# One layer's dense expert stage: every second V block in plain float32 instead of every sixth

## The chip, the cores and the metric

The kernel runs on one core of one Trainium2 chip. The metric is the device time of one execution in microseconds; the median of three runs of the kernel before is 4275.73 (4273.55 to 4280.51).

## What is computed

Two layers of a backbone over 512 latent tokens and 256 context tokens with 1024 features. Each layer has a token mixer and then PEER, a retrieval of small experts; the change touches PEER of the first layer alone. There each token gets, for each of 8 heads, the 16 best of 128 x 128 experts. Their rows of one table give activations, and the activations, weighted by a softmax gate, combine the rows of a second table:

```python
gate = jax.nn.softmax(top_s, axis=-1).astype(xb.dtype)
act = jax.nn.gelu(jnp.einsum('td,thkd->thk', xb, u_tab[eid]))
return jnp.einsum('thk,thkd->td', gate * act, v_tab[eid])
```

Each table has 16384 rows of 1024 floats, 64 MB a layer.

## The kernel before, in words

Tokens of a layer go one of two ways. The **dense** way (`peer_x`, line 1158) takes the first 384 of the 512 latent tokens of layer 0 against all 16384 experts, in 128 blocks of 128 experts. `ublock` (line 1200) loads a block of the transposed first table, multiplies it with the tokens and leaves GELU activations in one of 64 slots (32 in the tile `PA`, 32 in `PB`). `weights` (line 1211) builds one-hot matrices on VectorE and ScalarE, multiplies them on TensorE (tile `pwt`, line 1239), and so multiplies the slots by each token's gate; it is called 144 times in the layer, in three groups of 48. `vblock` (line 1245) loads a block of the second table and adds slot x block to the accumulators `dacc` (three of 128 tokens by 1024). U blocks run 64 ahead of V blocks, so in the stage looked at here one U block follows each of the first 64 V blocks, and the last 64 V blocks stand alone.

The **gather** way (`gtile_u`, line 1101, and `gtile_v`, line 1112) takes the other 128 latent tokens and the 256 context tokens. For each of 128 chosen experts a token, GpSimd issues an indirect load of 128 table rows (512 KB, tile `grow`, five buffers, line 1097); VectorE then multiplies and sums it (line 1108) or adds it to an accumulator (line 1121). One such load with its VectorE step is called a gather here. There are 768 in layer 0, of which 338 lie ahead of V block 0 in VectorE's order.

A float32 product is done in one of two ways. `block` (line 1192) loads 512 KB into `uv` (two buffers) and calls `split` (line 111): ScalarE writes a rounded part `uvh`, VectorE the remainder `uvl` (two buffers each). For a V block `split` is called a second time, for the slot's 384 columns (`wh`, `wl`). `mm` (line 116) then makes three passes of rounded float32 instead of one exact product: 18 matmuls for a V block. This is called a split block here. In a **plain** block (lines 1247 to 1250) nothing is split; `uv` and the slot go to TensorE as they are, with 6 float32 matmuls. A split block gives its `uv` buffer back when VectorE has written `uvl`, a plain block when TensorE has run its matmuls.

The order of the work on each engine is fixed when the kernel is built: a scheduler walks through all instructions by the levels that `prio` gives (line 81: 3 for the dense stage of layer 0, 6 for the gathers), and places them as its own estimates of durations have them come free. Each engine then executes its list in order, and waits where a semaphore is not there yet. Loads of `uv` are issued from SyncE. When the last V block is done, `L1304` and `L1146` write the layer's output for the 384 tokens, and layer 1 begins with a normalization, transposes and the input projection `pwin`.

Of the kernel before, what the change touches and what calls it, by code (L numbers as in the profile page):

```python
# [71 lines left out]
class Kern:  # L72
# [100 lines left out]
    def schedule(self):  # L173
        a = self.a
        with ExitStack() as er:
            ec = ExitStack()
            self.context(ec, 0)
            with self.banks("ctx0", "right", w=2, S=1) as ps, ExitStack() as e0:
                md = e0.enter_context(self.pool("mod", side="right"))
                pm = e0.enter_context(self.banks("mod", "right", w=1))  # L180
                fl = e0.enter_context(self.pool("flt"))
                pf = e0.enter_context(self.banks("flt", "left", w=2, S=1))
                with self.prio(1), ExitStack() as e:
                    self.filters(fl, pf, 0, LC)
                    self.modulation(md, pm, 0, 0, 2)
                    st = self.front(e, ps, ps, 0, 1, 1, side="right")
                    self.filters(fl, pf, 0, LX)
                    self.modulation(md, pm, 0, 2, 6)
                    self.back(ps, ps, 0, 1, st, None)
                    self.filters(fl, pf, 1, LX)  # L190
                    self.modulation(md, pm, 1, 0, 2)
            self.gp = er.enter_context(self.pool("gath", side="right"))
            with self.prio(1), self.banks("rc", "right", w=2) as ps:
                gc = self.route(ps, 0, 1, "GG", side="right")
            with self.banks("x0", "left", w=2, S=2) as ps:
                with ExitStack() as e:
                    with self.prio(3):
                        pr = e.enter_context(self.banks("x0b", "right", w=2))
                        st = self.front(e, ps, pr, 0, 0, 3, split=False)
                        ex = ExitStack()  # L200
                        self.back(ps, pr, 0, 0, st, ex)
                ec.close()
            with self.prio(6):
                self.gtile_u(0, gc[0])
                self.gtile_v(0, 1, 0, gc[0])
                self.gtile_u(0, gc[1])
            with self.prio(3):
                gx, ex = self.peer_x(0, 384, 6, 32, 32, (36, 46, 46), ex)
            with self.prio(6):
                self.gtile_u(0, gx[3])  # L210
                self.gtile_v(0, 0, 3, gx[3])
                self.gtile_v(0, 1, 1, gc[1])
            with ExitStack() as ec, ExitStack() as e:
                self.context(ec, 1)
                ps = e.enter_context(self.banks("x1", "left", w=2, S=2))
                pr = e.enter_context(self.banks("x1b", "right", w=2))
                with self.prio(3):
                    st = self.front(e, ps, pr, 1, 0, 4, ctx=True)
                with self.prio(4):
                    self.back(ps, pr, 1, 0, st, None, (2, 6))  # L220
            with self.prio(5):
                gx, _ = self.peer_x(1, 320, 0, 32, 46, (44, 42, 42), ex)
            with self.prio(6):
                for i in sorted(gx, reverse=True):
                    self.gtile_u(1, gx[i])
                    self.gtile_v(1, 0, i, gx[i])
# [1211 lines left out]
```

## Time and profile before

| | us |
|---|---|
| median of three runs (lowest, highest) | 4275.73 (4273.55, 4280.51) |
| the profiled execution | 4275.16 |
| its span, first to last instruction | 4273.3 |
| TensorE busy | 3707.9 (87%) |
| VectorE busy | 3510.8 (82%) |
| ScalarE busy | 1904.1 (45%) |
| GpSimd busy | 1532.1 (36%) |

The profile tells, for the whole span or for a stretch, how long each engine was busy, which TensorE clock was granted (1.00 is full speed), and the share of time in which the 16 DMA engines moved data. A list in order of time gives start and duration of single instructions, and in brackets how long the engine had been idle and what ended it. Matmuls overlap, so the price of one is the distance between starts.

### The profile page before, as it was taken

How to read it: one execution, taken by the hardware profiler on the slowest of the kernel's cores; microseconds unless marked ns; L12 is line 12 of the kernel's file. 1: busy time of each engine (PE TensorE's matmuls, PEld its weight loads, DVE VectorE, ACT ScalarE, POOL GpSimd, SP SyncE). 2: the span in 40 equal slices, each digit the busy share in tenths (PEclk: the TensorE clock that was granted, in tenths of full speed). 3: DMA queues.
4: the chain of work that ended last, by engine and by line, in shares of the span. 5: the costliest groups of instructions: out<-in, count | busy, mean ns of one | idle time of the engine just before them, and what ended most of it. 6: DMA issues, size and time to landing. Idle time of an engine off the chain costs nothing.

```text
span 4273.3 us, 63792 instructions
## 1 busy us (share of the span) xinstructions
PE 3707.9 (87%) x22514; PEld 2805.8 (66%) x22514; DVE 3510.8 (82%) x7449; ACT 1904.1 (45%) x3719; POOL 1532.1 (36%) x1225
## 2 busy tenths in 40 slices
PE   6887987968978989999969978888888999999997
PEld 3545544558878877877646656447878877776654
DVE  5746988889889889988898875755898998898988
ACT  5544243433257426622552244533334655555632
POOL 0000245642344563366436620000126345553243
PEclk7998998988999999999989989898999999999998
DMA  6654587885767897799879952242459788887697
GB/s 208 211 192 157 202 304 252 286 299 187 257 224 258 311 348 254 249 359 352 286 233 346 342 190 82 92 134 100 136 180 352 265 300 299 287 302 277 226 349 269
DMA packets 305635, 1063.74 MB, mean 249 GB/s; under 512 B 35757, under 2 KB 42625, under 8 KB 305315
## 3 DMA queue, kind: packets, MB, share of 16 engines
q0 software_dynamic: 165888, 604.05, 40.6%
q1 hardware_dynamic: 139426, 455.61, 30.6%
q8 instruction: 177, 2.90, 0.3%
q14 instruction: 144, 1.17, 0.1%
HBM read 1042.69 MB, written 16.84 MB: 248 GB/s over the span
## 4 chain that ended last, share of the span: by engine, by line
PE 32%; DMA 22%; DVE 17%; issue 16%; POOL 7%; ACT 5%; SPq 0%; POOLq 0%; DVEq 0%; ACTq 0%
PE pst L121 7%; POOL grow L1097 7%; DMA grow<-in_peer_v_dram,eid 6%; PE dacc L121 6%; DMA grow<-in_peer_u_dram,eid 6%; DMA uv<-in_peer_ut_dram 4%; PE pwin L121 4%; PE ppq L121 3%; DMA uv<-in_peer_v_dram 3%; DVE uvl L114 3%; DVE acc L1108 2%; DVE acc L1121 2%; PE pwo L121 2%; DMA wmod<-in_w_mod_dram 1%; ACT uvh L113 1%
## 5 line engine op out<-in xcount | busy, mean ns | idle before, releaser
L1097 POOL DMA_INDIRECT grow<-in_peer_u_dram,eid x576 | 747.8, 1298 | 1157.3 <-DVE acc L1108 566.4
L1097 POOL DMA_INDIRECT grow<-in_peer_v_dram,eid x576 | 776.6, 1348 | 746.4 <-DVE acc L1121 601.0
L121 PE MATMUL pst<-dhT,uvh 128*128 128x384 f32 (+1 forms) x4096 | 1001.6, 329 | 0.0
L113 ACT CAST uvh<-uv 128x1024 fp32r<-128x1024 f32 x491 | 513.0, 1045 | 680.5 <-DMA uv<-in_peer_v_dram 411.3
L121 PE MATMUL pst<-dhT,uvl 128*128 128x384 f32 (+1 forms) x2048 | 696.8, 340 | 112.3 <-DVE uvl L114 77.2
L1121 DVE SCALAR_TENSOR_TENSOR acc<-grow,gate,acc 128x1024 f32<-128x1024 f32 x571 | 732.2, 1282 | 53.8 <-DMA grow<-in_peer_v_dram,eid 46.0
L1108 DVE SCALAR_TENSOR_TENSOR acc<-grow,ghx 128x1024 f32<-128x1024 f32 x576 | 704.1, 1222 | 75.3 <-DMA grow<-in_peer_u_dram,eid 68.1
L121 PEld LDWEIGHTS pst<-dhT,uvh 128*128 128x128 f32 x4096 | 733.0, 193 | 4.1 <-issue 1.9
L114 DVE TENSOR_TENSOR uvl<-uv,uvh 128x1024 fp32r<-128x1024 f32 x491 | 599.1, 1222 | 159.5 <-ACT uvh L113 152.9
L121 PEld LDWEIGHTS pst<-dhT,uvl 128*128 128x128 f32 x2048 | 395.8, 193 | 212.3 <-DVE uvl L114 155.5
L121 PE MATMUL dacc<-uvh,wl 128*128 128x512 f32 x1154 | 481.2, 417 | 38.4 <-DVE wl L114 19.1
L121 PE MATMUL dacc<-uvl,wh 128*128 128x512 f32 x1154 | 467.3, 405 | 25.2 <-DVE uvl L114 25.1
L121 PE MATMUL dacc<-uvh,wh 128*128 128x512 f32 x1154 | 462.8, 401 | 0.0
L1235 ACT ACTIVATE o<-iota,di2n 128x128 f16<-128x128 f32 x1056 | 325.6, 390 | 28.8 <-PE pwt L1239 28.5
L121 PEld LDWEIGHTS dacc<-uvh,wl 128*128 128x128 f32 x1154 | 220.3, 191 | 128.4 <-ACT uvh L113 30.6
L121 PEld LDWEIGHTS dacc<-uvl,wh 128*128 128x128 f32 x1154 | 220.6, 191 | 82.7 <-DVE uvl L114 38.3
L121 PEld LDWEIGHTS dacc<-uvh,wh 128*128 128x128 f32 x1154 | 220.8, 191 | 48.3
L1239 PEld LDWEIGHTS <-o 128*128 128x128 f16 x4224 | 126.1, 97 | 110.7 <-issue 32.7
L1239 PE MATMUL pwt<-og,o 128*128 128x46 f16 (+3 forms) x4224 | 152.0, 182 | 43.3 <-DVE og L1225 35.5
L1205 ACT ACTIVATE PA<-pst 128x384 f32<-128x384 f32 (+1 forms) x128 | 59.5, 464 | 281.0 <-PE pst L121 280.9
L1205 ACT ACTIVATE PB<-pst 128x384 f32<-128x384 f32 (+1 forms) x128 | 59.2, 462 | 232.4 <-PE pst L121 231.8
L254 POOL MEMSET rmod<- 128x512 f32 (+1 forms) x8 | 3.3, 417 | 420.3 <-PE lpg L722 99.7
(399 smaller groups left out, 6092.6 us busy)
## 6 DMA issues: line engine op xcount, KB each, us to landing
uv<-in_peer_ut_dram SPq DMA_DIRECT2D x256, 512.0 KB
uv<-in_peer_v_dram SPq DMA_DIRECT2D x256, 512.0 KB
wmod<-in_w_mod_dram SPq DMA_DIRECT2D x96, 512.0 KB
wpq<-in_peer_wq_dram SPq DMA_DIRECT2D x48, 512.0 KB
w_in<-in_w_in_dram SPq DMA_DIRECT2D x72, 256.0 KB
w_in<-in_w_in_dram SPq DMA_DIRECT2D x18, 512.0 KB
grow<-in_peer_u_dram,eid POOLq DMA_INDIRECT x576
grow<-in_peer_v_dram,eid POOLq DMA_INDIRECT x576
```

The costliest lines, as they stand in the source:

```text
L113: self.nc.scalar.copy(hi, src)
L114: self.nc.vector.tensor_tensor(lo, src, hi.bitcast(F32), op=ALU.subtract)
L121: self.nc.tensor.matmul(p, w[i], x[j], start=start and n == 0, stop=stop and n == len(passes) - 1)
L254: nc.gpsimd.memset(r, 0.0)
L1097: self.nc.gpsimd.indirect_dma_start(out=r, out_offset=None, in_=self.a[table], in_offset=bass.IndirectOffsetOnAxis(ap=eid[:, j:j + 1], axi ...
L1108: nc.vector.scalar_tensor_tensor(junk, r, 1.0, hx, op0=ALU.mult, op1=ALU.mult, accum_out=dot[:, j:j + 1])
L1121: nc.vector.scalar_tensor_tensor(acc, r, w[:, j:j + 1], acc, op0=ALU.mult, op1=ALU.add)
L1205: nc.scalar.activation(slot(i), p, AF.Gelu_apprx_tanh)
L1235: nc.scalar.activation(o2[:, q], self.iota, AF.Abs, bias=i2n[:, t, k * NC + q:k * NC + q + 1])
L1239: nc.tensor.matmul(p[:, q, :], o2[:, q, :], og[:, g, q, :], start=(g == 0), stop=(g == 1))
```

## The change

The third argument of `peer_x`, `vn`, goes from 6 to 2 in layer 0. In `vblock` the plain way is taken if `i % vn == vn - 1`: 64 of the 128 V blocks in place of 21. Nothing else is edited.

```diff
             with self.prio(3):
-                gx, ex = self.peer_x(0, 384, 6, 32, 32, (36, 46, 46), ex)
+                gx, ex = self.peer_x(0, 384, 2, 32, 32, (36, 46, 46), ex)
```

The branch that takes the argument is not edited:

```python
if vn and i % vn == vn - 1:
    raw = dn.tile([128, D], F32, name="uv", bufs=2 + l)
    nc.sync.dma_start(raw, a["peer_v"][r0:r0 + 128, :])
    v, w = [raw], [slot(i)]
else:
    raw, v = block("v", a["peer_v"][r0:r0 + 128, :])
    w = [sp.tile([128, nd * 128], F32R, name=n, bufs=2) for n in ("wh", "wl")]
    self.split(*w, slot(i)[:, :nd * 128])
```

The scheduler places other instructions too. On VectorE, around V block 26, where `weights` (L1220, L1231, L1225, L1242) and gathers (L1108) are mixed with the splits (L114), before, from the `wl` of block 26 on:

```order
L114 TENSOR_TENSOR wl<-PA,wh 128x384
L1108 SCALAR_TENSOR_TENSOR acc,dot<-grow,ghx 128x1024
L1242 SCALAR_TENSOR_TENSOR PB<-pwt,PB 128x28x8
L1242 SCALAR_TENSOR_TENSOR PA<-pwt,PA 128x18x8
L1242 SCALAR_TENSOR_TENSOR PB<-pwt,PB 128x28x8
L1242 SCALAR_TENSOR_TENSOR PA<-pwt,PA 128x18x8
L1225 TENSOR_TENSOR og<-o_15149,diT 128x736
L114 TENSOR_TENSOR uvl<-uv,uvh 128x1024
```

and, in the change, a piece of the same place:

```order
L1108 SCALAR_TENSOR_TENSOR acc,dot<-grow,ghx 128x1024
L1225 TENSOR_TENSOR og<-o_14813,diT 128x736
L1108 SCALAR_TENSOR_TENSOR acc,dot<-grow,ghx 128x1024
L1220 TENSOR_TENSOR o_14846<-iotah,diT 128x368
L114 TENSOR_TENSOR uvl<-uv,uvh 128x1024
L1108 SCALAR_TENSOR_TENSOR acc,dot<-grow,ghx 128x1024 x3
L1242 SCALAR_TENSOR_TENSOR PB<-pwt,PB 128x28x8
```

In the change more gathers stand between the same `weights` steps: from V block 26 to V block 28 there were 3 gathers before, and there are 8 now.

On VectorE, at the end of the stage, the last gathers (L1121), splits (L114) and the first steps of the output (L1304, L1146, and L105 of layer 1's normalization), before:

```order
L1121 SCALAR_TENSOR_TENSOR acc<-grow,gate,acc 128x1024 x4
L114 TENSOR_TENSOR uvl<-uv,uvh 128x1024
L1121 SCALAR_TENSOR_TENSOR acc<-grow,gate,acc 128x1024 x3
L1304 TENSOR_TENSOR PA<-dacc_10704,PA 128x1024
L1304 TENSOR_TENSOR PA<-dacc_10705,PA 128x1024
L1146 TENSOR_TENSOR xs<-PA 128x1024 x2
L1304 TENSOR_TENSOR PA<-dacc_10706,PA 128x1024
L1121 SCALAR_TENSOR_TENSOR acc<-grow,gate,acc 128x1024
L1146 TENSOR_TENSOR xs<-PA 128x1024
```

and in the change, from V block 106 to V block 112 (the rows after these, up to `L1304`, are `wl` and `uvl` alone):

```order
L1121 SCALAR_TENSOR_TENSOR acc<-grow,gate,acc 128x1024 x6
L114 TENSOR_TENSOR uvl<-uv,uvh 128x1024
L114 TENSOR_TENSOR wl<-PB,wh 128x384
L1121 SCALAR_TENSOR_TENSOR acc<-grow,gate,acc 128x1024 x5
L1130 TENSOR_TENSOR acc<-acc,grow 128x1024
L114 TENSOR_TENSOR wl<-PB,wh 128x384
L114 TENSOR_TENSOR uvl<-uv,uvh 128x1024
L1146 TENSOR_TENSOR grow<-grow,acc 128x1024
```

The 768th gather of the layer stands ahead of V block 108's `wl` in the change; before, 749 stood ahead of `L1304`, and 19 followed it among the first steps of layer 1.

On SyncE, the loads of `uv` near the end of the stage and what each waits for (L1196 is a split block, L1249 a plain one; DVE is VectorE's `uvl`, PE the last matmul of a plain block), before:

```order
L1249 DMA uv<-in_peer_v_dram 128x1024 [waits DMAHW5_49,DVE_49]
L1196 DMA uv<-in_peer_v_dram 128x1024 [waits DMAHW6_49,DVE_49]
L1196 DMA uv<-in_peer_v_dram 128x1024 [waits DMAHW0_49,DVE_49]
L1196 DMA uv<-in_peer_v_dram 128x1024 [waits DMAHW7_49,PE_49]
L1196 DMA uv<-in_peer_v_dram 128x1024 [waits DMAHW1_49,DVE_49]
```

and in the change:

```order
L1249 DMA uv<-in_peer_v_dram 128x1024 [waits DMAHW3_49,DVE_49]
L1196 DMA uv<-in_peer_v_dram 128x1024 [waits DMAHW2_49,PE_49]
L1249 DMA uv<-in_peer_v_dram 128x1024 [waits DMAHW5_49,DVE_49]
L1196 DMA uv<-in_peer_v_dram 128x1024 [waits DMAHW4_49,PE_49]
L1249 DMA uv<-in_peer_v_dram 128x1024 [waits DMAHW7_49,DVE_49]
```

Every load of a split block now waits for TensorE; before, one in six did.

## Rows read from the trace of the kernel before

**Rows 1.** The page's first line, and busy time by stretch, stretches A to G.

```profile
span 4273.3 us, 63792 instructions
...
core 0: us, PE busy (x) PEld busy (x) DVE busy (x) ACT busy (x) POOL busy (x), PEclk, DMA share, GB/s
1432.60:1629.70 197.10, 173.62 (x831) 143.64 (x831) 163.96 (x250) 59.18 (x90) 123.82 (x92) 0.97 0.95 344
1629.70:1794.70 165.00, 162.89 (x1395) 137.29 (x1394) 156.07 (x324) 116.82 (x257) 53.06 (x41) 1.00 0.70 235
1794.70:2080.90 286.20, 260.15 (x1180) 217.54 (x1179) 243.22 (x262) 80.41 (x109) 188.14 (x135) 0.96 0.95 350
2080.90:2228.40 147.50, 109.71 (x1080) 78.62 (x1078) 141.13 (x278) 101.67 (x239) 32.75 (x34) 0.87 0.69 222
2228.40:2352.20 123.80, 113.00 (x413) 79.77 (x414) 104.46 (x99) 28.59 (x39) 81.10 (x59) 0.96 0.95 344
2352.20:2461.00 108.80, 98.95 (x369) 68.37 (x367) 92.25 (x87) 24.73 (x33) 67.11 (x51) 1.00 0.93 338
2461.00:2510.70 49.70, 19.02 (x69) 14.34 (x68) 48.25 (x75) 24.36 (x54) 19.27 (x20) 0.62 0.77 266
```

**Rows 2.** Stretches A, B, D and G, instructions on gathers alone (tile grow).

```profile
core 0: us, DVE busy (x) ACT busy (x) POOL busy (x), PEclk, DMA share, GB/s
1432.60:1629.70 197.10, 112.07 (x182) 0.00 (x0) 123.82 (x92) 0.97 0.95 344
1629.70:1794.70 165.00, 49.12 (x80) 0.00 (x0) 53.06 (x41) 1.00 0.70 235
...
2080.90:2228.40 147.50, 47.13 (x37) 0.00 (x0) 32.75 (x34) 0.87 0.69 222
...
2461.00:2510.70 49.70, 26.69 (x21) 0.00 (x0) 19.07 (x16) 0.62 0.77 266
```

**Rows 3.** VectorE in order of time, splits and a gather, from 2438.99.

```profile
start us, us, engine line op out<-in xcount [idle before <-releaser]
2438.99 1.22 DVE L114 TENSOR_TENSOR uvl<-uv,uvh 128x1024 fp32r<-128x1024 f32 x1
2440.13 0.55 DVE L114 TENSOR_TENSOR wl<-PB,wh 128x384 fp32r<-128x384 f32 x1
2440.60 1.28 DVE L1121 SCALAR_TENSOR_TENSOR acc<-grow,gate,acc 128x1024 f32<-128x1024 f32 x1
2441.79 0.55 DVE L114 TENSOR_TENSOR wl<-PB,wh 128x384 fp32r<-128x384 f32 x1
```

**Rows 4.** TensorE in order of time: a plain block and what follows; a split block likewise.

```profile
1479.01 5.31 PE L121 MATMUL dacc<-uv,PA 128*128 128x512 f32 x12
...
1484.69 0.33 PE L121 MATMUL pst<-dhT,uvl 128*128 128x384 f32 x1
...
1901.60 0.39 PE L121 MATMUL dacc<-uvh,wl 128*128 128x512 f32 x1
...
1905.81 0.33 PE L121 MATMUL pst<-dhT,uvl 128*128 128x384 f32 x1
...
1906.34 0.35 PE L121 MATMUL pst<-dhT,uvl 128*128 128x384 f32 x1
...
1910.00 5.31 PE L121 MATMUL dacc<-uv,PB 128*128 128x512 f32 x12
```

**Rows 5.** One load of uv, issued on SyncE and met by ScalarE's cast.

```profile
1926.53 0.33 SPq L1196 DMA_DIRECT2D uv<-in_peer_ut_dram  x1
1933.99 1.06 ACT L113 CAST uvh<-uv 128x1024 fp32r<-128x1024 f32 x1 [2.47 <-DMA uv<-in_peer_ut_dram]
```

**Rows 6.** Waits, 1434 to 2460 us: us in total, times, longest.

```profile
ACT uvh L113 <- DMA uv<-in_peer_v_dram: 293.2, 70, 8.8
POOL grow L1097 <- DVE acc L1121: 215.3, 111, 8.9
```

**Rows 7.** TensorE in order of time, layer 1's first projection matmul.

```profile
2497.93 0.80 PE L121 MATMUL pwin<-hT,w_inl 128*128 128x512 f32 x1 [3.14 <-ACT hT L113]
```

## The prediction

> **What bounds the kernel now.** I read the busy time by stretch first. I cut the dense stage of layer 0 where VectorE writes `wl` for V blocks 0, 20, 36, 66, 82 and 108, and where the last block ends: A to F in [rows 1]; G, 50 us, is the start of layer 1. Three different limits show. In A, C, E and F the DMA engines are busy 93 to 96% and move 338 to 350 GB/s, whatever else the stretch does. In B, with 45 `weights` steps, TensorE is busy 162.9 of 165.0 us and VectorE 156.1, and DMA only 70%. In D, with 48, VectorE is busy 141.1 of 147.5 us. In G it is busy 48.3 of 49.7 us, 26.7 of them on gathers [rows 1, 2], while TensorE waits until 2497.93 for its first projection matmul [rows 7]. The time per 512 KB transfer says the same: C holds 136 gathers, 30 V and 28 U blocks (counted in VectorE's order, by the `uvl` and `wl`), 194 transfers in 286.2 us, 1.475 us each; E holds 58 + 26 = 84 in 123.8 us, 1.474 each.
>
> So the stage is a list in fixed order over three resources that are all nearly full, and what counts is which work stands together. The gathers cost VectorE and DMA but no TensorE; the dense blocks cost all three.
>
> **What the change removes and adds.** 43 V blocks become plain. Each loses a `uvl` and a `wl` on VectorE: by distance of starts 1.14 and 0.47 us [rows 3], 1.61 together, 69 us in all. ScalarE loses two casts a block; it is idle for more than half of A, C, E and F [rows 1], so I cost that at nothing; if a cast were late, TensorE would wait, and that wait only shrinks. TensorE pays: from the first matmul of a plain block to the second `uvl` pass of the U block behind it are 1484.69 - 1479.01 = 5.68 us, behind a split block 1906.34 - 1901.60 = 4.74 [rows 4]. A split block itself takes 1905.81 - 1901.60 = 4.21, so a plain one takes 4.21 + 0.94 = 5.15, a U block 1910.00 - 1905.81 = 4.19. That is 40 us more on TensorE. DMA bytes are unchanged: plain or split, a block is one 512 KB load.
>
> In the plain matmul the trace has two records, 5.31 us for twelve, some 0.4 us apart, against three passes of 0.234 us. The Trainium skill (FP8 and Floating Point Precision, TensorE Precision Notes) says that true FP32 takes four passes through the array; four at the split pass's distance would make a plain block 5.6 us and the extra 1.41, not 0.94, 60 us in all and some 5 more in F. The trace disagrees, and the sum uses the trace.
>
> **Where it lands** follows from the new order of VectorE, which moves gathers more than it removes splits. By stretch, between the same V blocks (U blocks likewise counted in the order):
>
> A (V 0 to 20): 91 + 20 + 18 = 129 transfers before, 93 + 20 + 15 = 128 now. TensorE needs 20 x 4.68 (the mean of 4.21 and 5.15) + 15 x 4.19 = 156 us, below the 197. Full of DMA as before: 0.
>
> B (20 to 36): gathers go from 40 to 65, `weights` steps from about 45 to 48, `uvl` from 30 to 28, `wl` from 13 to 8. A gather costs 49.12 / 40 = 1.23 us of VectorE here [rows 2], a `weights` step (156.1 - 49.1 - 34.2 - 6.1) / 45 = 1.48. VectorE: 156.1 + 30.8 + 4.4 - 2.3 - 2.4 = 186.6 us. TensorE: 162.9 + 5 x 0.94 + 3 U blocks x 4.19 + about 2 for `weights` (a matmul group of it: an estimate from 16 short matmuls) = 182. At 97% busy, between today's 95% of VectorE and 99% of TensorE, that is 193: **+28**.
>
> C (36 to 66): 147 + 30 + 26 = 203 transfers against 194. 203 x 1.475 = 299: **+13**. VectorE and TensorE both stay below (some 240 and 249).
>
> D (66 to 82): 56 gathers against 35, 12 `uvl` against 16, 8 `wl` against 14. VectorE 141.1 + 21 x 1.19 [rows 3] - 4.6 - 2.8 - 2.4 (two sums of a tile's output that move elsewhere) = 156.3; at today's 95.7% that is 163: **+16**.
>
> E (82 to 108): 69 + 26 = 95 transfers against 84: 140 us by DMA. But here a `uv` buffer becomes tight. On SyncE each split load waits for a plain block's last matmul, and each plain load for the `uvl` of the split block ahead of it. So one pair's chain is: load, cast and subtract (1.05 + 1.14 and some 0.2 between), load, plain matmuls 5.15; per four blocks, as the two buffers alternate, 2L + 7.5 us. The load in [rows 5] took L = 1933.99 - 1926.53 = 7.5 us under traffic: 22.5 us, and for 26 blocks 146: **+22**. The same chain in C is four loads per eight V and U blocks, 4L + 12.4 = 42.4 us, which the 299 us allow (42.7), so it adds nothing there.
>
> F (108 to the end): 51 gathers before, none now. The loads alone (20 of them) leave DMA free, so TensorE sets the pace: stretch F holds 369 matmul records, 1.5 blocks more than its own 20 (17 x 18 + 3 x 12 = 342). 21.5 x 4.68 = 101 against 108.8: **-8**.
>
> G: the 19 gathers that delayed layer 1's first steps are gone. VectorE loses 26.7 of 48.3 busy us there. Bounds: 0, if ScalarE's stretch of statistics (24.4 us busy in G, much of it in sequence) already sets the pace, and -26.7. I take two thirds, since VectorE was 97% busy: **-18**. What is late next is that chain itself. Behind G the engines' orders are the same in both kernels, so nothing else changes.
>
> Sum: 0 + 28 + 13 + 16 + 22 - 8 - 18 = **+53 us** on the profiled execution's 4275.2 (span 4273.3 [rows 1] and about 2 around it; 0.6 below the median): **4328 us**. The lesson in it: 69 us leave VectorE, but the new order spends them at once on gathers placed earlier, at places where DMA or VectorE is full, and leaves the last 20 blocks on TensorE alone, with DMA two thirds idle.
>
> **Rivals.**
> 1. *Faster: the full stretches are not at a DMA ceiling but at the pace at which VectorE frees `grow` buffers.* GpSimd waited 215 us for VectorE's accumulations [rows 6], which speaks for it. Then A, C and E fall until TensorE limits: A 156 / 0.95 = 165 (-32), C 249 / 0.96 = 260 (-26), E 26 x 4.68 = 122 (-2). With B, D, F and G as above: -42, **4233 us**. It decides if a transfer comes below about 1.35 us in those stretches: 426 transfers by 0.12 us are the 53. Against it: four stretches with different mixes agree on 338 to 350 GB/s [rows 1]. The Trainium skill (HBM Reference, Specifications) puts about 425 GB/s for a core that streams alone, and 358 as its share when its neighbour streams too; at 425 a transfer would be 1.23 us and this rival right. No stretch of this trace comes near it. 8%.
> 2. *Slower still: the buffer chain decides.* A cast waited up to 8.8 us for a V load [rows 6], so L can be at least that. Then E is 26 / 4 x 25.1 = 163 (+39, not +22), C 56 / 8 x 47.6 = 333 (+47, not +13), A 35 / 8 x 47.6 = 208 (+11): 62 more, **4390 us**, and up to 35 more if F also keeps such loads. Against it: L is long only while the queue is full, and a late load empties it. 15%.
> 3. *No change:* the extra gathers in B and D fit into gaps (44 us less) and G gives 26.7. Then it is 4275. Both would need VectorE at 100% and more, so 7%.
>
> That the change does not do what it says is excluded: its order has 64 plain loads in layer 0.
>
> **How the numbers follow.** The forecast gets 70%, with its own range 4291 to 4360 (B and D at half and G at -26.7; L a little longer). The range reaches from **4285 to 4390**: of the fast rival nothing, of no change little, of the buffer chain the near half, which leaves out under 2 in 10. About 0.2% (8.5 us) is what a measurement of this kernel can tell from no change. Faster takes rival 1, **0.08**; within 0.2%, most of rival 3, **0.05**; slower **0.87**.
>
> **What would show it.** In the profile after: TensorE's total some 40 us up; `uvl` 448 and `wl` 192 in place of 491 and 235. B and D with VectorE at 95% or more and longer by 28 and 16 us. A, C and E at 340 to 350 GB/s. The last 100 us of the stage without gathers, DMA at about a third, TensorE over 95%. Layer 1's first projection matmul some 20 us after the last block instead of 37. It is wrong if A, C or E move above 370 GB/s (rival 1), or fall below 320 with casts waiting longer for V loads (rival 2), or if F's TensorE has gaps.

## The result, and the profile after

| | before | after |
|---|---|---|
| median on the same chip, six runs each | 4273.21 (4257.70 to 4280.51) | 4347.70 (4334.18 to 4354.36) |
| span of the profiled execution | 4273.3 | 4347.1 |
| TensorE busy | 3707.9 | 3769.0 |
| VectorE busy | 3510.8 | 3444.5 |
| gathers in A, B, C, D, E, F, behind F | 91, 40, 136, 35, 58, 51, 19 | 93, 65, 147, 56, 69, 0, 0 |

The changed kernel takes 1.018 times as long (95% interval 1.0162 to 1.0197): 74.5 us more by the medians, where 53 were forecast.

The page of the changed kernel first: the span, the engines' totals, and the two groups of the split.

```profile
span 4347.1 us, 63024 instructions
...
PE 3769.0 (87%) x22256; PEld 2772.0 (64%) x22256; DVE 3444.5 (79%) x7363; ACT 1840.7 (42%) x3633; POOL 1487.1 (34%) x1225
...
L113 ACT CAST uvh<-uv 128x1024 fp32r<-128x1024 f32 x448 | 467.6, 1044 | 789.9 <-DMA uv<-in_peer_v_dram 503.3
L114 DVE TENSOR_TENSOR uvl<-uv,uvh 128x1024 fp32r<-128x1024 f32 x448 | 547.1, 1223 | 240.0 <-ACT uvh L113 236.4
```

The change does what it says: 448 `uvl` where there were 491, and VectorE 66 us less busy. TensorE is 61 us busier. The number to stop at stands at the end of the `uvh` row: the idle time ahead of the cast that loads of V blocks ended is 503.3 us. In the page of before the same row ends in 680.5 and 411.3, with 491 casts. Fewer casts, and more waiting for their loads.

Busy time by stretch in the changed kernel, cut at the same V blocks as [rows 1]. F ends and G begins where VectorE starts the layer's output (`L1304`); TensorE's last matmul ends 3.4 us later here, at 2549.7, and within 0.4 us of it before. The last row is G, here up to 2584.6.

```profile
core 0: us, PE busy (x) PEld busy (x) DVE busy (x) ACT busy (x) POOL busy (x), PEclk, DMA share, GB/s
1435.20:1623.40 188.20, 163.33 (x666) 125.15 (x665) 147.59 (x223) 38.36 (x53) 118.61 (x92) 0.95 0.95 345
1623.40:1828.90 205.50, 192.30 (x1490) 148.19 (x1489) 184.48 (x380) 120.47 (x270) 80.89 (x68) 0.99 0.80 273
1828.90:2131.30 302.40, 264.62 (x1066) 200.52 (x1065) 243.33 (x227) 61.98 (x86) 183.25 (x146) 0.94 0.96 350
2131.30:2305.20 173.90, 128.61 (x1096) 83.11 (x1094) 157.06 (x285) 96.01 (x231) 55.75 (x57) 0.85 0.76 253
2305.20:2444.10 138.90, 121.48 (x355) 69.90 (x355) 106.66 (x94) 15.66 (x23) 84.82 (x66) 0.93 0.93 340
2444.10:2546.30 102.20, 102.20 (x330) 62.10 (x329) 19.49 (x23) 15.50 (x20) 0.00 (x0) 1.00 0.34 114
2546.30:2584.60 38.30, 21.92 (x73) 15.05 (x72) 24.56 (x53) 24.59 (x56) 0.20 (x4) 0.64 0.27 83
```

Against [rows 1]: A is 9 us shorter, B 40 longer, C 16, D 26, E 15, F 6 shorter. The stage starts 2.6 later, and what follows the start of the output takes 1800.8 us instead of 1812.7 (before, it starts at 2460.6). B and D carry 67 of the 74. In both no resource is full: VectorE is busy 184.5 of 205.5 us in B and 157.1 of 173.9 in D, 90% each, where it had 95 and 96%; TensorE is busy 94% of B, where it had 99%.

What B waited for, before (165 us) and after (205.5 us); columns as in [rows 6].

```profile
ACT uvh L113 <- DMA uv<-in_peer_v_dram: 10.6, 4, 3.6
ACT uvh L113 <- DMA uv<-in_peer_ut_dram: 7.8, 7, 3.4
DVE uvl L114 <- ACT uvh L113: 4.6, 5, 1.7
```

```profile
ACT uvh L113 <- DMA uv<-in_peer_ut_dram: 28.8, 10, 7.6
ACT uvh L113 <- DMA uv<-in_peer_v_dram: 25.7, 7, 8.2
DVE uvl L114 <- ACT uvh L113: 16.9, 12, 3.5
```

The casts of a 205 us stretch wait 54.5 us for their 512 KB loads, where they waited 18.4, and VectorE stands behind the cast for 16.9 instead of 4.6. DMA is busy only 80% of B, so a full queue is not the whole reason. In F, with DMA at 34%, a cast that waits meets its load 3.2 us after the issue (issued at 2474.94, cast at 2478.15); for the 17 casts of B that wait it is 5.7 us on average. What is left of the wait is a load issued late. How long SyncE (SPq) waited for TensorE's V blocks in B before it issued such a load, before and after:

```profile
SPq L1196 <- PE dacc L121: 8.0, 2, 4.5
```

```profile
SPq L1196 <- PE dacc L121: 31.7, 9, 5.9
```

(That every load of a split block waits for TensorE holds where V blocks stand alone; in B, where U blocks share the two buffers, it is about one in three.) A piece of C shows how, in order of time: loads on SyncE, a plain block on TensorE, and one cast that waits for its load.

```profile
1991.49 0.33 SPq L1249 DMA_DIRECT2D uv<-in_peer_v_dram  x1
...
1996.47 0.33 SPq L1196 DMA_DIRECT2D uv<-in_peer_ut_dram  x1
...
2000.79 5.31 PE L121 MATMUL dacc<-uv,PB 128*128 128x512 f32 x12
...
2003.85 1.04 ACT L113 CAST uvh<-uv 128x1024 fp32r<-128x1024 f32 x1 [7.54 <-DMA uv<-in_peer_ut_dram]
...
2006.17 0.33 SPq L1196 DMA_DIRECT2D uv<-in_peer_v_dram  x1
```

The plain block is loaded at 1991.49 and read by TensorE until 2006.10; the next load into its buffer goes out at 2006.17. For these 14.7 us every other load has to use the one buffer that is left. The load issued into that one at 1996.47 is met by its cast 7.4 us later, and ScalarE had been idle 7.54 us for it. Whether such waits are what makes B long is not settled by the profile of the change; the run with a third buffer bears on it. Over the stage, 1435 to 2540, the waits of the changed kernel are:

```profile
ACT uvh L113 <- DMA uv<-in_peer_v_dram: 373.3, 59, 12.2
...
ACT uvh L113 <- DMA uv<-in_peer_ut_dram: 165.6, 42, 7.9
...
DVE uvl L114 <- ACT uvh L113: 146.7, 64, 7.8
```

539 us of the casts' idle time end with a load. Before, it was 293.2 for loads of V blocks [rows 6], and for those of U blocks

```profile
ACT uvh L113 <- DMA uv<-in_peer_ut_dram: 90.6, 43, 7.5
```

384 in all, with more casts to wait. Of layer 1, the first projection matmul:

```profile
2574.45 0.79 PE L121 MATMUL pwin<-hT,w_inl 128*128 128x512 f32 x1 [2.00 <-ACT hT L113]
```

It stands 28 us behind the start of the output, where it stood 37 behind [rows 7]; behind TensorE's last matmul it is 25 us, and was 37.

### The profile page after: what moved, and what is told of

It reads as the page before. It is cut to its first block, busy times and chain, and to the rows that moved or that the text cites. A ratio compares the mean times of both kernels' runs of the same rounds, so it can differ in the third digit from the quotient of the medians.

```text
span 4347.1 us, 63024 instructions
## 1 busy us (share of the span) xinstructions
PE 3769.0 (87%) x22256; PEld 2772.0 (64%) x22256; DVE 3444.5 (79%) x7363; ACT 1840.7 (42%) x3633; POOL 1487.1 (34%) x1225
## 4 chain that ended last, share of the span: by engine, by line
PE 32%; DMA 25%; DVE 17%; issue 15%; POOL 6%; ACT 5%; SPq 0%; POOLq 0%; DVEq 0%; ACTq 0%
PE dacc L121 7%; DMA grow<-in_peer_u_dram,eid 7%; PE pst L121 6%; DMA grow<-in_peer_v_dram,eid 6%; POOL grow L1097 6%; DMA uv<-in_peer_ut_dram 4%; DMA uv<-in_peer_v_dram 4%; PE pwin L121 4%; PE ppq L121 3%; DVE uvl L114 3%; DVE acc L1108 2%; DVE acc L1121 2%; ACT uvh L113 1%; PE pwo L121 1%; PE fp L412 1%
## 5 line engine op out<-in xcount | busy, mean ns | idle before, releaser
L1121 DVE SCALAR_TENSOR_TENSOR acc<-grow,gate,acc 128x1024 f32<-128x1024 f32 x571 | 733.1, 1284 | 89.2 <-DMA grow<-in_peer_v_dram,eid 81.8
L113 ACT CAST uvh<-uv 128x1024 fp32r<-128x1024 f32 x448 | 467.6, 1044 | 789.9 <-DMA uv<-in_peer_v_dram 503.3
L1108 DVE SCALAR_TENSOR_TENSOR acc<-grow,ghx 128x1024 f32<-128x1024 f32 x576 | 704.7, 1224 | 77.2 <-DMA grow<-in_peer_u_dram,eid 71.8
L114 DVE TENSOR_TENSOR uvl<-uv,uvh 128x1024 fp32r<-128x1024 f32 x448 | 547.1, 1223 | 240.0 <-ACT uvh L113 236.4
L121 PE MATMUL dacc<-uvh,wl 128*128 128x512 f32 x896 | 387.8, 433 | 45.9 <-ACT uvh L113 43.3
L121 PE MATMUL dacc<-uvl,wh 128*128 128x512 f32 x896 | 370.8, 414 | 27.5 <-DVE uvl L114 27.4
L121 PE MATMUL dacc<-uvh,wh 128*128 128x512 f32 x896 | 363.8, 406 | 0.0
L121 PEld LDWEIGHTS dacc<-uvh,wl 128*128 128x128 f32 x896 | 174.5, 195 | 125.9 <-ACT uvh L113 61.0
L121 PEld LDWEIGHTS dacc<-uvl,wh 128*128 128x128 f32 x896 | 174.9, 195 | 81.3 <-DVE uvl L114 44.0
L121 PEld LDWEIGHTS dacc<-uvh,wh 128*128 128x128 f32 x896 | 175.3, 196 | 37.9
L121 PE MATMUL dacc<-uv,PA 128*128 128x512 f32 x384 | 181.0, 610 | 5.8 <-DMA uv<-in_peer_v_dram 5.7
L121 PE MATMUL dacc<-uv,PB 128*128 128x512 f32 x384 | 176.1, 608 | 8.4 <-DMA uv<-in_peer_v_dram 8.4
```

What stands on the lines that cost most here:

```text
L113: self.nc.scalar.copy(hi, src)
L114: self.nc.vector.tensor_tensor(lo, src, hi.bitcast(F32), op=ALU.subtract)
L121: self.nc.tensor.matmul(p, w[i], x[j], start=start and n == 0, stop=stop and n == len(passes) - 1)
L1108: nc.vector.scalar_tensor_tensor(junk, r, 1.0, hx, op0=ALU.mult, op1=ALU.mult, accum_out=dot[:, j:j + 1])
L1121: nc.vector.scalar_tensor_tensor(acc, r, w[:, j:j + 1], acc, op0=ALU.mult, op1=ALU.add)
```

## The experiments

What the forecast left unproved is why B and D grew. **The first theory** is the forecast's: the new order puts gathers where VectorE or DMA are full. **Its rival**: the plain block itself costs, whatever the order, since it runs longer on TensorE and keeps its `uv` buffer until TensorE has read it. All edits are to the changed kernel unless said otherwise; ratios are to the kernel before on the same chip.

### The VectorE work put back: e1_keep_splits

```diff
                     v, w = [raw], [slot(i)]
+                    if i % 6 != 5:
+                        junk = [dn.tile([128, D], F32R, name=n, bufs=2) for n in ("uvh", "uvl")]
+                        self.split(*junk, raw)
+                        junk = [sp.tile([128, nd * 128], F32R, name=n, bufs=2) for n in ("wh", "wl")]
+                        self.split(*junk, slot(i)[:, :nd * 128])
```

> 64 plain V blocks on TensorE as in the change, but the 43 new ones are still split on ScalarE and VectorE; the parts are written and not used. So TensorE's extra work and the longer hold of the uv buffer stay, VectorE's 69 us are not freed, and the scheduler spreads the gathers nearly as before: 482, 620, 659 and 721 stand ahead of V blocks 36, 66, 82 and 108 (change 496, 643, 699, 768; before 469, 605, 640, 698), and gathers reach to the end of the stage. Theory (the new place of the gathers is the loss): B about +25, D +7, E +6, F -8, G -12: about 4288 us. Rival 1 (the plain blocks themselves cost it, TensorE or the buffer): as the change or slower, 4345 us or more, since VectorE is not relieved. Rival 2 (no gather behind the end matters most): between the two.

Measured: 4340.12 us, 1.0173 (1.014 to 1.0207), beside 1.018 for the change. The theory's time missed by over 50 us, the rival's by 5. With the splits put back the time is the same, to within some 16 us. That does not make the 69 us worthless by themselves, for the order moved halfway back with them (gathers 88, 56, 138, 39, 62 in A to E): against the change D is 13 us shorter and F, which has gathers again, 21 longer. What the run shows is that the relief and the places that the scheduler gave it are together worth nothing. B has the VectorE work of the change.

```profile
1612.50:1820.10 207.60, 197.01 (x1494) 151.21 (x1493) 184.56 (x376) 129.61 (x282) 71.61 (x58) 0.97 0.73 245
```

In this B stretch VectorE is busy 184.6 of 207.6 us, 89%, with nine gathers fewer than the change has there.

### The plain product taken away: e2_no_plain_cost

```diff
+            last = []
...
-                    v, w = [raw], [slot(i)]
+                    v, w = last if i % 6 != 5 else ([raw], [slot(i)])
...
+                    last[:] = v, w
```

> The other half: for the 43 new plain blocks nothing is split, but TensorE repeats the 18 rounded passes of the split block before (so those blocks' own values are loaded and left out of the sum, and the block before counts twice). VectorE is relieved as in the change, TensorE pays nothing extra, and a uv buffer is not held for a matmul. Gathers again move ahead: 485, 632, 682, 749 ahead of V blocks 36, 66, 82, 108, all 768 ahead of block 118. Theory: still slower, B +33, C +13, D +21, E +13, F -18, G -12: about 4323 us. Rival 1 (the plain blocks' own cost): at or under the time before, 4273 us or less, since the relief stays and the cost goes.

Measured: 4293.73 us, 1.0065 (1.0045 to 1.0084): 28 us more than before. It lies between the two: the theory's 4323 is too high, the rival's 4273 too low. With VectorE relieved, and neither longer matmuls nor a held `uv` buffer, the kernel is still slower than before. Its order (88, 59, 147, 50, 67 gathers in A to E) is left to do it, and one thing that the edit itself brings: TensorE reads the split parts of a block twice, so `uvh` and `uvl` come back later. Over the stage the casts wait 68.0 us for TensorE to give `uvh` back, where they waited 40.2 before. How much of the 28 us that is, no run tells. Its stretches B and C:

```profile
1614.50:1803.00 188.50, 185.19 (x1532) 155.60 (x1531) 178.48 (x368) 120.14 (x270) 77.29 (x61) 0.99 0.80 274
1803.00:2112.70 309.70, 270.01 (x1180) 227.35 (x1179) 242.12 (x239) 64.97 (x90) 195.86 (x146) 0.93 0.94 344
```

B without the hold runs as the forecast had it run, VectorE busy 95%, TensorE 98%, and 23.5 us longer than before, though with 59 gathers and not the change's 65.

### The hold alone: e5_hold_only

On top of that edit, one tiny matmul that reads the plain block's `uv`, so that the buffer is again held until TensorE comes to it:

```diff
+                if l == 0 and i % 2 == 1 and i % 6 != 5 and i < 127:
+                    nc.tensor.matmul(acc[2][:, 1016:1024], slot(i)[:, 0:128], raw[:, 0:8], start=False, stop=False)
```

> As e2 (for the 43 new plain blocks nothing is split and TensorE repeats the 18 rounded passes of the split block before), and one matmul of 8 columns reads the block's own uv buffer behind them, so that the buffer is held until TensorE is through, as in the change (output again not the sum asked for, and the 8 columns add to it). VectorE's order is that of the change within a few gathers (493, 647, 698, 765 ahead of V blocks 36, 66, 82, 108). What it lacks of the change is TensorE's 0.94 us a block. Buffer theory (the held uv buffer leaves TensorE without the next block, and its clock falls): 4325 us or more, e2's 4294 plus at least 30. TensorE theory (the six float32 matmuls cost it): e2's 4294 plus about 5 for the small matmuls. Order theory: 4305, for the gathers stand a little further ahead than in e2.

Measured: 4344.10 us, 1.0148 (1.0126 to 1.0169). That is 0.83% above the run without the hold: 35 us, some 12 either way. (The small matmul reads the block's slot too, which e2 leaves unread, so a later return of the slot is in this figure.) Its stretches B and C:

```profile
1620.10:1828.30 208.20, 189.82 (x1545) 157.70 (x1544) 184.19 (x378) 120.86 (x270) 84.30 (x67) 0.99 0.76 259
1828.30:2159.20 330.90, 276.96 (x1193) 231.50 (x1192) 253.76 (x238) 65.41 (x88) 197.84 (x153) 0.91 0.92 335
```

B grew from 188.5 to 208.2, with TensorE down from 98 to 91% and VectorE from 95 to 88%. The waits of the stage, 1435 to 2540, first without and then with the hold:

```profile
ACT uvh L113 <- DMA uv<-in_peer_v_dram: 199.7, 35, 17.4
...
ACT uvh L113 <- DMA uv<-in_peer_ut_dram: 63.6, 27, 8.1
```

```profile
ACT uvh L113 <- DMA uv<-in_peer_v_dram: 335.3, 55, 11.7
...
ACT uvh L113 <- DMA uv<-in_peer_ut_dram: 56.2, 35, 4.8
```

The casts wait 391 us for loads instead of 263. The 35 us are not all wait, though: the scheduler answered the hold with another order, three gathers more in A, five in B and seven in C. VectorE is 5.7 us busier in B, and ten transfers at the forecast's 1.475 us are 15 in A and C. That leaves some 15 us, an estimate, for the hold itself. By stretch, A to F, the profile with the hold is longer by 5, 20, 21, 3, -3 and -1 us: the hold strikes in B and C, hardly in D. And in B it does not work through late casts: these wait 29 us for loads with the hold and 20 without, and VectorE waits 3.6 and 3.5 us for them.

### A third buffer: e6_third_uv_buffer and e7_29_slots

A third `uv` buffer fits only if `PB` has 29 slots instead of 32; e7 has the 29 slots with two buffers, e6 with three.

```diff
-                gx, ex = self.peer_x(0, 384, 2, 32, 32, (36, 46, 46), ex)
+                gx, ex = self.peer_x(0, 384, 2, 32, 29, (36, 46, 46), ex)
```

and, in e6 alone, at both places:

```diff
-                    raw = dn.tile([128, D], F32, name="uv", bufs=2 + l)
+                    raw = dn.tile([128, D], F32, name="uv", bufs=3)
```

> The change with three uv buffers in layer 0 in place of two; to make room, PB has 29 slots in place of 32 (U blocks run 61 ahead of V blocks instead of 64). Gathers ahead of V blocks 36, 66, 82, 108: 492, 640, 713, 768. Buffer theory: casts no longer wait for loads behind plain blocks; against e7 30 to 50 us less, 4295 to 4315 us. TensorE theory: as e7 within 10 us. Order theory: as e7 within 10 us.

> Control for e6: the change with two uv buffers as it is and PB of 29 slots. All theories: as the change, 4335 to 4355 us.

Measured: 4349.78 (1.0162, 1.0145 to 1.0179) with three buffers and 4375.97 (1.0221, 1.0204 to 1.0238) with two. The 29 slots alone cost more than was expected, 0.41% over the change, 17 us with some 10 either way; D takes 205 us in e7 and 174 in the change. The third buffer gives back 0.59%, 25 us with some 10 either way; the orders of the two are nearly the same (gathers in A to E 93, 64, 148, 73, 55 and 93, 65, 147, 71, 57), so this comparison is the cleanest on buffers. The casts' waits for loads in the stage, e6 and then e7:

```profile
ACT uvh L113 <- DMA uv<-in_peer_v_dram: 139.7, 24, 12.7
...
ACT uvh L113 <- DMA uv<-in_peer_ut_dram: 13.0, 3, 4.9
```

```profile
ACT uvh L113 <- DMA uv<-in_peer_v_dram: 345.0, 53, 12.3
...
ACT uvh L113 <- DMA uv<-in_peer_ut_dram: 175.0, 47, 9.7
```

520 us fall to 153, and the time falls by 25. Most of those waits were hidden behind other work; about one microsecond in fifteen of them was on the path. In part they also moved to the next pair of buffers: over the stage the casts of e6 wait 112.0 us for TensorE to give `uvh` back, a wait that e7 does not have. By stretch, A to F, e6 is longer than e7 by 2, -7, -12, -4, -3 and -8 us.

B is the stretch to look at. Its row in e6, and what VectorE waited for there:

```profile
1612.30:1817.80 205.50, 194.26 (x1487) 150.77 (x1487) 184.74 (x378) 120.85 (x272) 81.92 (x66) 0.98 0.77 265
```

```profile
DVE acc L1108 <- DMA grow<-in_peer_u_dram,eid: 10.2, 10, 2.6
...
DVE PB L1242 <- PE pwt L1239: 6.8, 11, 1.5
...
DVE uvl L114 <- ACT uvh L113: 0.2, 1, 0.2
```

No cast of this stretch waits for a load any more, and VectorE no longer waits for casts. Yet B takes 205.5 us, as in the change, with VectorE again at 90%: it now waits for the loads of gathers and for TensorE's `weights` matmuls. Against the 212.8 us of e7 that is 7 us less. So the late loads are a small part of what makes B long. What the change and e6 have in common there is the order and TensorE's work, 192 and 194 us of busy time.

### The third buffer in the kernel before: e8_third_uv_before

Both edits of e6, with `vn` at 6.

> The kernel before (every sixth block plain) with three uv buffers and 29 slots. Buffer theory: there are still 21 held buffers and the stretches A, C, E, F are at 340 to 350 GB/s; e3 without any plain block showed 356 there and 33 us less, so about 4245 us. TensorE and order theory: as before, 4265 to 4275 us.

Measured: 4279.20, 1.0001 (0.999 to 1.0012); the expected gain did not come. If 29 slots cost as much here as in the change, the buffer paid for them and no more; a run with 29 slots and two buffers at `vn` 6 was not made, so how much a third buffer is worth in the kernel before is open. By stretch, A and C are 7 and 11 us shorter than before, as expected of them, and what follows the stage 14; D, which has 57 gathers in place of 35, is 34 us longer.

### No plain block at all: e3_no_plain and e12_no_plain_again

```diff
-                gx, ex = self.peer_x(0, 384, 2, 32, 32, (36, 46, 46), ex)
+                gx, ex = self.peer_x(0, 384, 0, 32, 32, (36, 46, 46), ex)
```

> No plain block at all in layer 0. The scheduler then leaves more gathers for later: 457, 586, 620, 671 ahead of V blocks 36, 66, 82, 108, and 58 of the 768 behind the last block (19 before). Theory: the dense stage ends some 40 us earlier than in the kernel before (about 2420 us) and the start of layer 1 gets that back, G some 45 to 55 us longer: 4273 to 4290 us. Rival 1 (each plain block costs by itself, 1.7 us as in the change's 43): 21 fewer make it 36 us faster, about 4237 us.

> e3 once more, beside e11 on one chip: 0.5 to 1.0% under the kernel before.

Measured: 4235.23 (0.9925, 0.9898 to 0.9952) and 4248.50 (0.9928, 0.9905 to 0.9951): 31 us faster than before. The theory had 4273 to 4290 for the first; the rival, at a flat price of 1.7 us a plain block, had 4237. The time thus climbs from none to 21 to 64 plain blocks by 31 and by 77 us, 1.5 and 1.8 us a block, though VectorE is relieved by 1.61 each time. Stretches A, C and D of the first run:

```profile
1429.70:1609.80 180.10, 168.16 (x864) 144.71 (x863) 159.92 (x242) 64.11 (x97) 116.76 (x85) 1.00 0.96 356
...
1768.70:2047.50 278.80, 260.12 (x1326) 223.24 (x1324) 248.86 (x298) 98.14 (x145) 181.63 (x129) 1.00 0.96 356
2047.50:2179.80 132.30, 96.02 (x976) 70.31 (x976) 132.30 (x260) 94.06 (x221) 31.40 (x33) 0.87 0.69 214
```

A and C move 356 GB/s, with TensorE's granted clock at 1.00 where before had 0.97 and 0.96 [rows 1] and the change 0.95 and 0.94. D is the other extreme: VectorE has no idle time at all, and TensorE is busy 73%. That is the one place where VectorE's time should be worth buying.

### Where a plain block pays: e4, e9, e10, e11

Four kernels with plain blocks in chosen stretches, by the condition in `vblock` and with `vn` at 6:

```diff
-                if vn and i % vn == vn - 1:
+                if vn and (i % vn == vn - 1 or 66 <= i < 82):
```

for e4, and likewise `or (i < 66 and i % 2)` for e9, `or (i >= 82 and i % 2)` for e10; for e11 the condition is `66 <= i < 82` alone.

> Plain blocks as before (every sixth), and besides all 16 V blocks of stretch D (66 to 81), where VectorE was busy 96% and TensorE 74%. 14 more plain blocks free 22.5 us of VectorE there and cost TensorE 13 us. C and D together hold 26 gathers more, F 7 fewer, G none. Theory: D +8 to +15, F -8, G -12: 4262 to 4273 us, a little faster than before. Rival 1 (plain blocks cost by themselves 1.7 us): 4297 us.

> Every second V block plain below block 66, every sixth from there on: 43 plain blocks, 22 more than before. Gathers ahead of blocks 36, 66, 82, 108: 496, 643, 687, 745, none behind the end. A flat price per plain block (the change lost 1.7 us for each of 43): 22 x 1.7 = 37 us more than before. Local theory (the price is paid where all three resources are short, B with its 16 blocks, and where the buffer is held in A and C): A, B and C as in the change, together 47 us longer, D with 44 gathers some 10 longer, E and F shorter since fewer gathers are left (about -5 and -12), G -12: 25 to 35 us more than before.

> Every sixth V block plain below block 82, every second from there on: 36 plain blocks, 15 more than before. VectorE's order is the one of before up to block 82; 709 gathers ahead of block 108 (698 before), 768 at the end (749). A flat price per plain block: 15 x 1.7 = 26 us more than before. Local theory: E +14 and F +5 by the buffer and the transfers, G -12: within 10 us of before.

> Plain blocks in stretch D alone (V blocks 66 to 81, all 16), none elsewhere. In e3 VectorE was busy all of D's 132.3 us and TensorE 96. 26 us of VectorE leave D. Gathers: 643 ahead of block 82 (e3: 620), 735 ahead of the end (e3: 710), so 33 remain for layer 1's start in place of 58. A flat price per plain block: e3 + 16 x 1.7, 27 us over it. Local theory: at e3 or up to 20 us below it, that is 0.5% to 1.2% under the kernel before.

| | plain blocks against | us, ratio (interval) | a block |
|---|---|---|---|
| e9 | before: 22 more in A to C | 4340.67, 1.0142 (1.0114 to 1.017) | +2.8 |
| e10 | before: 15 more behind block 82 | 4286.93, 1.0028 (1.0013 to 1.0042) | +0.8 |
| e4 | before: 14 more in D | 4258.80, 0.9973 (0.9958 to 0.9988) | -0.8 |
| e11 | none: the 16 of D alone | 4226.45, 0.9886 (0.9863 to 0.991) | -1.1 |

The last column is the ratio's distance from the kernel named (e11's from the 0.9928 of e12), times 4274 us, by the number of blocks. There is no flat price. The 22 early blocks cost 61 us, more than either side had expected (37, or 25 to 35); with the 12 us of the 15 late ones that is 73, near the 77 us of the whole change, which has 6 more in D. (That the sum comes so near is in part luck: e9 and e10 each contain a gain behind the stage, 12 and 16 us by their profiles, that the whole change has once.) With plain blocks in D the sign turns: e4 and e11 are faster than the kernels they stand against. In e4's profile the stage is 5 us longer than before and what follows it 19 shorter, with none of the 19 gathers left behind. Where e11's gain comes from, the stage as a whole and layer 1's projection tell, first without plain blocks (e3), then in e11. The stretch row runs from V block 0 to the start of the output behind the last; in the row on `pwin`, the last two times are the starts of the first and the last of these 288 matmuls.

```profile
1429.70:2389.10 959.40, 882.41 (x5378) 731.68 (x5377) 883.44 (x1296) 439.67 (x808) 512.04 (x372) 0.98 0.87 311
```

```profile
L121 PE MATMUL pwin<-hT,w_inh x288: 387/389/796, 2429.2 to 2584.4; 128*128 128x512 f32 x144
```

```profile
1429.40:2401.30 971.90, 895.67 (x5282) 718.37 (x5281) 889.09 (x1290) 419.57 (x776) 542.64 (x397) 0.98 0.89 321
```

```profile
L121 PE MATMUL pwin<-hT,w_inh x288: 387/389/796, 2440.1 to 2571.8; 128*128 128x512 f32 x144
```

The stage is not shorter with e11's plain blocks but 12.5 us longer (3 us longer than in the profile of e12, the same kernel as e3, where the stage takes 969 us and what follows it 1844). GpSimd issues 397 times in it where it issued 372: VectorE's freed time took gathers that would otherwise stand among the first steps of layer 1. There they had cost more: the projection takes 155 us without plain blocks and 132 in e11, and all that follows the stage 1840.9 us and 1806.7. So the gain is real, but not where the plain blocks are. The same trade in the whole change had less to move: in the kernel before only 19 gathers stood behind the stage, and moving them gave 12 us. e11 is the fastest kernel of the study, 1.1% below the kernel before; against e12 its gain is 0.42%, 18 us with some 14 either way.

## Why the forecast held in direction and fell short in size

The time is 4347.7 where 4328 was forecast, inside the forecast's own range of 4291 to 4360. By its steps:

**Counts and prices: right.** VectorE's work came to 184.5 us in B and 157.1 in D; 186.6 and 156.3 were worked out. `uvl` is at 448, the gathers stand as the order said. F, with no gather, ran at DMA 34%, TensorE 100%, clock 1.00: from one plain block to the next, with a split block between, are 9.36 us, 4.68 a block, as the forecast had it:

```profile
2535.07 5.31 PE L121 MATMUL dacc<-uv,PB 128*128 128x512 f32 x12
...
2544.43 5.31 PE L121 MATMUL dacc<-uv,PB 128*128 128x512 f32 x12
```

The Trainium skill (FP8 and Floating Point Precision, TensorE Precision Notes) has true FP32 in four passes; by that, an estimate with the split pass's 0.234 us, the two blocks would take 9.83 us, and F again agrees with the shorter time.

**DMA's ceiling: right, and rival 1 fell with it.** A, C and E moved 345, 350 and 340 GB/s, and even without plain blocks 356. C came to +16 for +13. The Trainium skill (HBM Reference, Specifications) gives about 425 GB/s for a core that streams alone; no stretch of any run shown here comes near it.

**B, "At 97% busy, [...] that is 193": failed, 205.5.** So did **D, "at today's 95.7% that is 163"**: 173.9. Both took the work of the busiest engine by the share at which it ran before. VectorE's share fell to 90% in both. TensorE's part of B was also short: 192.3 us busy, where 182 were worked out. What took the share down is only in part known. The run without hold and long products has B at 188.5 with VectorE at 95%, and the hold alone takes it to 208.2; but with a third buffer, and no cast waiting for a load in B, it is 205.5 all the same. In D the hold alone does little: VectorE is busy 95% there without it (e2) and 94% with it (e5). In the change VectorE waits in D 9.2 us for casts, 3.6 before, and 4.8 for loads of gathers, none before; which edit does that was not taken apart. The terms of B and D were 12 and 10 us short, as much as the whole sum was. The rest nearly cancels: A came to -9 for 0 (it had been kept at its old 197.1 / 129 = 1.53 us a transfer, and ran at 188.2 / 128 = 1.47), C to +16 for +13, E to +15 for +22, F to -6 for -8, G to -12 for -18, and the stage starts 2.6 later.

**The buffer chain, "so it adds nothing there": right for C, and not asked of B.** The forecast worked the chain out as a rate for stretches full of DMA and gave it 6 us in E. E then stayed at the time of its transfers, 138.9 us, and C took 302.4 for the 299 of its own. For B the forecast did not ask what a held buffer does. Rival 2 named the mechanism, but put it in C, E and A, with 62 us more; the runs give the hold 35, some 15 of them beyond the gathers that move with it, most of it in B and C.

**G, -18: -12.** With the gathers gone ScalarE is busy 24.6 of 38.3 us there, and the first projection comes 25 us behind TensorE's last matmul, not some 20. Cut at that matmul, as the forecast had it, G is 15 us shorter and F 3.

**TensorE, +40 in total: +61.** The clock granted in A, C, D and E is lower by 0.02 to 0.03 than in [rows 1], and over the execution 0.934 for 0.938; 3708 us of busy time stretched by that ratio are some 16 more, an estimate.

By differences of runs, the 77 us (1.8% of 4274) divide so: 28, some 8 either way, for the new order with VectorE relieved (e2, with what its second reading of the split parts costs); 35, some 12 either way, for the hold, with the gathers that it moves; the other 14, again some 12 either way, for the longer products. The forecast's main reason, VectorE's freed time spent on gathers placed earlier, would thus be more than half of it, with the first 28 and perhaps 20 of the next 35, and not the whole. The runs differ in their orders as well, so this division is an estimate and not a proof. Why a block costs most in A to C is only argued: U and V blocks share the two buffers there, and in B TensorE and VectorE are both full. No run took that apart.

## What to carry to other kernels

An exchange of one engine's time for another's has no price of its own: the same edit cost 2.8 us a block in one stretch, 0.8 in another and gave about 1 in a third, where the relieved engine was at 100% and the loaded one at 73%, and even there the gain came behind the stage, from gathers taken out of layer 1's start. Ask of each stretch which engine is idle there, and try the exchange there alone. Count who gives a buffer back as part of an instruction's price: an operand that the matmul reads directly lives until the matmul, and the late load shows on another engine, as a cast that waits. But price such a wait by a run that removes it: in B a third buffer took the casts' waits for loads away, and with them 7 of 213 us. And where a scheduler orders the work, look at how it spends what was freed before counting it as gained.

## What was not expected

- The largest single relief had no worth as the scheduler spent it: with 69 us of splits put back, and the gathers halfway back with them, the time is 1.0173 of before, without them 1.018.
- The plain blocks that the kernel before already had cost it 0.7%; without them the granted clock in A and C is 1.00 and DMA moves 356 GB/s instead of 344 to 350.
- Three slots fewer of 64 cost 0.41% in the change.
- Waits of casts for loads may be long and nearly free: 367 us of them taken away were worth 25.
